# A two-layer diffusion trunk on one core: low parts of 28 second-layer weight chunks made one block earlier, and three modulations moved to TensorE

## The chip, the core and the metric

The kernel runs on one core of one Trainium2 chip. The core has TensorE for matrix products (PE, with its weight loads listed as PEld), VectorE (DVE), ScalarE (ACT), GpSimd (POOL) and SyncE (SP); here SP issues nearly all transfers, in the order in which they stand in its queue. Every engine works through its own instructions in the order of the program and waits for others on semaphores. The metric is the device time of one execution, in microseconds (us).

## The reference

Two layers of a diffusion trunk are computed for one sequence of 256 latent tokens and one of 256 context tokens, 1024 channels, all in float32. From a condition vector six modulations of 1024 values come per layer, `silu(c) @ w_ada + b_ada`. They shift, scale and gate:

```python
hl = modulate(x, ml[..., 0, :], ml[..., 1, :])
zl = hl @ w_in[l] + b_in[l]            # 1024 x 7680: q, k, v, conv, pool, gates
...
x = layer_norm(DEEPNORM_ALPHA * x + ml[..., 2, :] * mix(zl, attn_l), ln1_g[l], ln1_b[l])
x = layer_norm(DEEPNORM_ALPHA * x + ml[..., 5, :] * ffn(modulate(x, ml[..., 3, :], ml[..., 4, :])), ...)
```

`mix` joins attention, a 31-tap depthwise convolution branch and a pooling branch by gates and multiplies by `w_out`. `ffn` is `w_up` (1024 x 5632), a 3-tap depthwise convolution, a gate, and `w_down` (2816 x 1024). The first layer does all of it for both sequences. The second needs of the context only keys and values.

## The kernel before

**Weights are streamed.** All weights lie in memory as chunks of 128 x 1024 float32 (512 KB), in the order of the list `ORDER`. An item of it is ("conv", layer, j, half), ("kv", ...), ("q", ...), ("up", ...), ("down", ...) and so on. `load_to` issues the loads on SP some items ahead of their use (`LA` = 6) into six buffers called `raw`. A product in float32 is made of three products in a faster format, lines 362 to 364: high part of the one by high part of the other, low by high, high by low. So each chunk is split: ACT copies it to the short format (`hi`, line 260), and DVE subtracts (`lo = raw - hi`, line 261). `split_to` does this three chunks ahead of use, into five `hi` and five `lo` buffers. In the first layer one matmul covers 512 columns (both sequences), in the second 256 for most weights.

**Stages.** For each layer: 16 conv chunks, 4 kv, 8 q, then gates, pooling, attention and the output product; a layer norm; 44 up chunks; 22 down chunks; a layer norm. The 31 taps of the convolution (line 649, tiles `H`) are DVE work in the background. `run_bg` hands out a set number of them at each step (`NTAPS`), at a lower priority, so that a scheduler may put them later, and the order on DVE is then fixed when the program is built.

**Modulations** are made in two ways. `ada` (line 309) is a TensorE product: four matmuls of 32 columns by 256 for each of 8 chunks, then a copy of the row (DVE, line 315) and two transposes (line 343). `adt` (line 331) is a DVE product that is summed on the way, once or twice per chunk, from two buffers called `rawt`. `_ADA` and `_ADT` say which modulation is made how and in which phase. `adt` items are put in a list `due` as the use of the stream passes them, and `run_due` works them off, in the feed-forward blocks of the first layer. `take_ada` takes the modulation items that stand next in the stream, at a layer norm.

**Layer norms.** Residual sums are transposed (line 429), DVE takes means and variances, the normed tiles are transposed back (line 468), and ACT and DVE make the modulated high and low parts (`hh` line 500, `hl` line 505), which the first matmuls of the next stage need. The first three chunks of that stage are taken before the norm.

## Time and profile before

| what | value |
|---|---|
| median of 3 runs (lowest, highest) | 1458.98 us (1457.18, 1460.99) |
| profiled execution: its time / its span from first to last instruction | 1459.06 us / 1457.3 us |
| PE busy, share of the span | 1397.7 us, 96% |
| DVE busy | 1097.2 us, 75% |
| ACT busy | 700.4 us, 48% |
| mean granted TensorE clock | 0.987 |

The prediction cuts the span into stages, by the times at which tiles of that stage appear: the first feed-forward block's norm and up part (539 to 805), the norm before the second layer (923.3 to 945.7), its conv chunks (945.7 to 989.6), kv (989.6 to 1012.2), q and the start of attention (1012.2 to 1061.7), and gates, pooling and attention (1061.7 to 1171.5); its norm before the up part lies at 1242.5 to 1257. A window row gives for each engine the busy time in that stretch and the count of instructions, then the granted clock, the share of the 16 DMA engines and GB/s. Busy PE is not PE at its peak: it also counts pipelined time, so the count of matmuls per stretch is read beside it.

### The profile page before, as it was taken

How to read it: one execution, taken by the hardware profiler on the slowest of the kernel's cores; microseconds unless marked ns; L12 is line 12 of the kernel's file. 1: busy time of each engine (PE TensorE's matmuls, PEld its weight loads, DVE VectorE, ACT ScalarE, POOL GpSimd, SP SyncE). 2: the span in 40 equal slices, each digit the busy share in tenths (PEclk: the TensorE clock that was granted, in tenths of full speed). 3: DMA queues.
4: the chain of work that ended last, by engine and by line, in shares of the span. 5: the costliest groups of instructions: out<-in, count | busy, mean ns of one | idle time of the engine just before them, and what ended most of it. 6: DMA issues, size and time to landing. Idle time of an engine off the chain costs nothing. (4 is left out here: it accounts for less than half of the span.)

```text
span 1457.3 us, 21593 instructions
## 1 busy us (share of the span) xinstructions
PE 1397.7 (96%) x8340; PEld 1209.6 (83%) x8340; DVE 1097.2 (75%) x1999; ACT 700.4 (48%) x1162; POOL 62.0 (4%) x61
## 2 busy tenths in 40 slices
PE   7999899999999999999999999889799989899997
PEld 5777678888877898888888888887678989899997
DVE  3598896986994757777765866699999968777753
ACT  3332356554738437333333222643576765655542
POOL 0020320000000000000000000000400000000000
PEclk9999999999999999999999999999989999999999
DMA  9543332323232521444442777344323345355550
GB/s 365 208 178 132 111 109 73 94 101 100 98 122 94 187 88 71 155 153 150 159 153 82 254 245 241 114 144 165 121 95 124 123 160 188 129 181 183 177 171 29
DMA packets 64550, 212.28 MB, mean 146 GB/s; under 512 B 7360, under 2 KB 8512, under 8 KB 64320
## 3 DMA queue, kind: packets, MB, share of 16 engines
q1 hardware_dynamic: 62320, 207.95, 41.8%
q10 hardware_dynamic: 2128, 2.96, 0.6%
q8 instruction: 65, 1.06, 0.3%
q14 instruction: 37, 0.30, 0.1%
HBM read 209.83 MB, written 1.05 MB: 145 GB/s over the span
## 5 line engine op out<-in xcount | busy, mean ns | idle before, releaser
L260 ACT ACTIVATE hi<-raw 128x1024 fp32r<-128x1024 f32 (+2 forms) x295 | 303.8, 1034 | 481.9 <-PE mm L363 361.3
L261 DVE TENSOR_TENSOR lo<-raw,hi 128x1024 fp32r<-128x1024 f32 (+2 forms) x295 | 352.6, 1199 | 132.9 <-ACT hi L260 127.8
L363 PE MATMUL mm<-hl,hi 128*128 128x256 f32 (+1 forms) x1112 | 352.3, 319 | 2.5 <-DVE hl L505 2.4
L362 PE MATMUL mm<-hh,hi 128*128 128x256 f32 (+1 forms) x1112 | 348.1, 320 | 6.5 <-ACT sg L671 3.2
L364 PE MATMUL mm<-hh,lo 128*128 128x256 f32 (+1 forms) x1112 | 350.9, 317 | 2.7 <-DVE lo L261 2.7
L649 DVE SCALAR_TENSOR_TENSOR H<-gl,vt,H 128x502 f32<-128x502 f32 (+29 forms) x480 | 267.2, 614 | 0.1
L362 PEld LDWEIGHTS mm<-hh,hi 128*128 128x128 f32 x1112 | 211.4, 193 | 22.2 <-ACT sg L671 3.6
L363 PEld LDWEIGHTS mm<-hl,hi 128*128 128x128 f32 x1112 | 214.2, 193 | 18.2 <-DVE hl L505 3.8
L364 PEld LDWEIGHTS mm<-hh,lo 128*128 128x128 f32 x1112 | 214.2, 193 | 16.5 <-DVE lo L261 2.9
L362 PE MATMUL mm<-hi,hi 128*128 128x512 f32 x464 | 186.1, 401 | 0.0
L364 PE MATMUL mm<-hi,lo 128*128 128x512 f32 x368 | 144.5, 393 | 1.4 <-DVE lo L261 1.4
L363 PE MATMUL mm<-xlo,hi 128*128 128x512 f32 x368 | 144.0, 391 | 0.0
L362 PE MATMUL mm<-ah,hi 128*128 128x256 f32 (+1 forms) x374 | 123.1, 329 | 0.0
L364 PE MATMUL mm<-ah,lo 128*128 128x256 f32 (+1 forms) x374 | 122.8, 328 | 0.0
L363 PE MATMUL mm<-al,hi 128*128 128x256 f32 (+1 forms) x374 | 122.3, 327 | 0.0
L331 DVE CUSTOM_DVE_ANT_0 prod<-rawt,cb,vt 128x1024 f32<-128x1024 f32 x80 | 102.5, 1282 | 17.5 <-DMA rawt<-in_wst 16.6
L362 PEld LDWEIGHTS mm<-hi,hi 128*128 128x128 f32 x464 | 87.8, 189 | 25.0 <-issue 5.7
L364 PEld LDWEIGHTS mm<-hi,lo 128*128 128x128 f32 x368 | 69.1, 188 | 16.8 <-DVE lo L261 2.2
L363 PEld LDWEIGHTS mm<-xlo,hi 128*128 128x128 f32 x368 | 69.2, 188 | 13.9 <-issue 0.4
L364 PEld LDWEIGHTS mm<-ah,lo 128*128 128x128 f32 x374 | 71.1, 190 | 6.1
L363 PEld LDWEIGHTS mm<-al,hi 128*128 128x128 f32 x374 | 71.1, 190 | 6.0
L362 PEld LDWEIGHTS mm<-ah,hi 128*128 128x128 f32 x374 | 71.1, 190 | 5.9
(197 smaller groups left out, 2065.3 us busy)
## 6 DMA issues: line engine op xcount, KB each, us to landing
raw<-in_wst SPq DMA_DIRECT2D x296, 512.0 KB, 3.6
rawt<-in_wst SPq DMA_DIRECT2D x56, 512.0 KB, 4.1
ad<-in_wst SPq DMA_DIRECT2D x32, 256.0 KB, 6.0
raw<-in_wst SPq DMA_DIRECT2D x16, 384.0 KB, 3.2
x<-in_xT SPq DMA_DIRECT2D x8, 256.0 KB, 6.3
raw<-in_wst SPq DMA_DIRECT2D x8, 256.0 KB, 2.6
x<-in_xT ACTq DMA_DIRECT2D x8, 256.0 KB, 3.1
bq<-in_brow SPq DMA_DIRECT2D x6, 256.0 KB, 3.5
```

The costliest lines, as they stand in the source:

```text
L260: pin(A.activation(hi[:, :w], r[:, :w], AF.Copy))
L261: pin(V.tensor_tensor(lo[:, :w], r[:, :w], hi[:, :w].bitcast(F32), op=ALU.subtract))
L331: tc.keep_in_program_order(V.tensor_tensor_reduce(prod, w, cb[:, s], 1.0, col(l, "b_ada", m * 8 + c), ALU.mult, ALU.add, mods[l, m][:, c, ...
L362: pin(PE.matmul(ps, lh, rh, start=(first and i == 0), stop=False))
L363: pin(PE.matmul(ps, lh, rl, start=False, stop=False))
L364: pin(PE.matmul(ps, ll, rh, start=False, stop=(last and i == n - 1)))
L649: V.scalar_tensor_tensor(h[:, :, a:b], g[:, :, a + d:b + d], col(l, "dw_w", k * 8 + j), h[:, :, a:b], op0=ALU.mult, op1=ALU.add,)
```

## The change

**Low parts made early.** `PRE` lists the 28 chunks of layer 1's conv, kv and q. Each appears a second time in the stream, as ("pre", ...), spread over the up part of layer 0's feed-forward block: it is loaded there into a `rawt` buffer (three now), ACT makes its high part (in a `hi` buffer), DVE overwrites the chunk with its low part, and SP stores that to a scratch tensor in memory (`scr`). In layer 1, `split_to` then loads the low part from there instead of having DVE subtract it. The high part is made by ACT from the weights as before. `run_due` has a second place in the up loop.

**Modulations.** (0,5), (1,2) and (1,5) go from `adt` to `ada`. They are put behind the first three chunks of the up part of layer 0, of the conv of layer 1 and of the up part of layer 1, so `take_ada` takes them at the layer norms. (1,0), which is made for both sequences, goes from the up to the down part. `adt` products in the up part are 16 instead of 48, in the down part 32 as before.

**Buffers.** Five `raw` and three `rawt` instead of six and two; outside the stretch that has side items (`adt`, `pre`), the stream uses all eight in turn. Loads run 8 items ahead instead of 6.

```diff
-NRAW = 6
-NRAWT = 2
-LA = 6
+NRAW = 5
+NRAWT = 3
+LA = 8
...
-_ADA = {(0, "mix"): ((0, 2), (0, 4), (0, 3))}
-
-_ADT = {(0, "up"): ((0, 5), (1, 1), (1, 0)), (0, "down"): ((1, 2), (1, 4), (1, 3), (1, 5))}
+_ADA = {(0, "mix"): ((0, 2), (0, 4), (0, 3)), (0, "up"): ((0, 5),), (1, "conv"): ((1, 2),), (1, "up"): ((1, 5),)}
+
+_ADT = {(0, "up"): ((1, 1),), (0, "down"): ((1, 0), (1, 4), (1, 3))}
+
+PRE = [("conv", 1, j, h) for j in range(8) for h in range(2)] + [("kv", 1, k) for k in range(4)]
+PRE += [("q", 1, c, k) for c in range(2) for k in range(4)]
...
-    o = o[:GRP] + _spread(o[GRP:], ada)
+    o = o[:GRP] + ada["conv"] + _spread(o[GRP:], ada["mix"])
...
-    o += up[:GRP] + _spread(up[GRP:], adt["up"])
-    o += _spread([("down", l, c, p) for c in range(7) for p in range(3)], adt["down"])
+    o += up[:GRP] + ada["up"] + _spread(up[GRP:], _spread([("pre",) + it for it in PRE if l == 0], adt["up"]))
+    down = [("down", l, c, p) for c in range(7) for p in range(3)]
+    o += _spread(down[:18], adt["down"]) + down[18:]
...
-            if it[0] == "adt":
+            if it[0] in ("adt", "pre") or (not side(nxt["load"]) and nxt["load"] % (NRAW + NRAWT) >= NRAW):
                 t = wp.tile([P, CH], F32, tag="rawt", name=f"rawt{nxt['load']}", bufs=NRAWT)
...
             pin(A.activation(hi[:, :w], r[:, :w], AF.Copy))
-            pin(V.tensor_tensor(lo[:, :w], r[:, :w], hi[:, :w].bitcast(F32), op=ALU.subtract))
+            if it in scr:
+                load(lo[:, :w].bitcast(F32), scr.pop(it), False)
+            else:
+                pin(V.tensor_tensor(lo[:, :w], r[:, :w], hi[:, :w].bitcast(F32), op=ALU.subtract))
...
+    def pre(*it):
+
+        r = raw.pop(("pre",) + it)
+        hi = wp.tile([P, CH], F32R, tag="hi", name=uid("prehi"))
+        A.activation(hi, r, AF.Copy)
+        lo = r.bitcast(F32R)
+        tc.keep_in_program_order(V.tensor_tensor(lo, r, hi.bitcast(F32), op=ALU.subtract))
+        scr[it] = dp.tile([P, CH], F32, name=uid("scr"))
+        load(scr[it], r, False)
...
+            run_due(1)
             A.activation(acc[:, :T], acc[:, :T], AF.Silu)
```

The instructions move with it, in the order in which they stand on each engine. In these rows L362 to L364 before are L393 to L395 after, L261 is L281, L649 is L680, L673 is L704, L429 and L468 are L460 and L499, and L202 is L210.

**PE, from the last down product of layer 0 into layer 1's first conv chunks** (`ah`, `al`: activations; `sT`: residual sums; `nat`: normed tiles; `hh`: the modulated input). Before:

```order
L364 MATMUL mm940_7785<-ah908_6976,lo267_7678 128x256
L468 MATMUL ax950_7974<-ID_76,nat915_7186 128x128 x4
L468 MATMUL ax957_7993<-ID_76,nat927_7413 128x128 x2
L429 MATMUL ax948_7965<-ID_76,sT941_7852 128x128
L429 MATMUL ax948_7965<-ID_76,sT939_7747 128x128
```

After the change:

```order
L395 MATMUL mm999_7959<-ah965_7163,lo279_7858 128x256
L329 MATMUL ad1007_8144<-raw284_7855,sc_88 32x256 x3
L329 MATMUL ad1007_8144<-rawt285_7941,sc_88 32x256 x4
L329 MATMUL ad1007_8144<-rawt286_7947,sc_88 32x256 x4
L329 MATMUL ad1007_8144<-rawt287_7953,sc_88 32x256 x4
L329 MATMUL ad1007_8144<-raw288_8120,sc_88 32x256 x4
L329 MATMUL ad1007_8144<-raw289_8122,sc_88 32x256 x4
L329 MATMUL ad1007_8144<-raw290_8124,sc_88 32x256 x4
L374 MATMUL ax1009_8189<-ID_78,adarow1008_8187 128x128 x2
L460 MATMUL ax1010_8195<-ID_78,sT998_7927 128x128
```

27 of the 32 modulation matmuls and the two transposes of their row now stand between the last product and the norm's transposes, which the next stage's input waits for; the other five stand a little ahead, in the last product.

**DVE, in layer 1's conv chunks** (`gl`: the gated conv input; `H`: taps). Before:

```order
L261 TENSOR_TENSOR lo284_8595<-raw284_8485,hi284_8594 128x1024
L673 SCALAR_TENSOR_TENSOR gl1013_8625<-mm1010_8567,vt1_81,sg1012_8623 128x256
L261 TENSOR_TENSOR lo285_8653<-raw285_8516,hi285_8652 128x1024
L649 SCALAR_TENSOR_TENSOR H984_8166<-gl982_8131,vt1_81,H984_8166 128x247 x2
L649 SCALAR_TENSOR_TENSOR H984_8166<-gl982_8131,vt1_81,H984_8166 128x246 x2
L649 SCALAR_TENSOR_TENSOR H984_8166<-gl982_8131,vt1_81,H984_8166 128x245 x2
```

After the change:

```order
L704 SCALAR_TENSOR_TENSOR gl1075_8855<-mm1072_8797,vt1_83,sg1074_8853 128x256
L680 SCALAR_TENSOR_TENSOR H1046_8396<-gl1044_8361,vt1_83,H1046_8396 128x243 x2
L680 SCALAR_TENSOR_TENSOR H1046_8396<-gl1044_8361,vt1_83,H1046_8396 128x242 x2
L680 SCALAR_TENSOR_TENSOR H1046_8396<-gl1044_8361,vt1_83,H1046_8396 128x241 x2
L704 SCALAR_TENSOR_TENSOR gl1075_8855<-mm1081_8886,vt1_83,sg1074_8853 128x256
```

The subtractions are gone here, and taps move up. In DVE's order 83 taps stood ahead of layer 1's first kv bias addition (`nat<-mm,bq`), and 104 do now; ahead of the last rotated query tile it was 104 and is 124; ahead of the first pooled tile 144 and 148; ahead of the last 246 and 246.

**SP, in layer 0's up part.** Before, weight chunks (`raw`) and modulation chunks (`rawt`) alternate:

```order
L202 DMA rawt169_5783<-in_wst 128x1024
L202 DMA raw186_6211<-in_wst 128x1024
L202 DMA rawt172_5859<-in_wst 128x1024
L202 DMA raw187_6213<-in_wst 128x1024
L202 DMA rawt175_5937<-in_wst 128x1024
```

After the change:

```order
L210 DMA scr824_5660<-rawt160_5204 128x1024
L210 DMA raw180_5842<-in_wst 128x1024
L210 DMA rawt166_5536<-in_wst 128x1024
L210 DMA scr828_5671<-rawt162_5216 128x1024
L210 DMA raw182_5875<-in_wst 128x1024
L210 DMA rawt168_5587<-in_wst 128x1024
```

Stores of low parts stand between the loads. A store waits for DVE, and the next load of the same buffer (`rawt168` takes the place of `rawt162`) waits for the store. In layer 1's conv part SP's order then has one raw chunk and one low part by turns:

```order
L210 DMA rawt301_8505<-in_wst 128x1024
L210 DMA lo296_8508<-scr863_6077 128x1024
L210 DMA rawt302_8552<-in_wst 128x1024
L210 DMA lo297_8555<-scr867_6088 128x1024
L210 DMA rawt303_8583<-in_wst 128x1024
L210 DMA lo298_8586<-scr872_6163 128x1024
```

A low part's load waits there until PE has done with the chunk five places before it, whose buffer it takes; the raw loads run eight chunks ahead.

More of the change, by code (lines that the diff above doesn't have):

```diff
@@ L92, in weight_order @@
     o += [("pw", l, c) for c in range(8)]
-    ada = [("ada", a, m, k) for a, m in _ADA.get((l, "mix"), ()) for k in range(KT)]
+    ada = {
+        ph: [("ada", a, m, k) for a, m in _ADA.get((l, ph), ()) for k in range(KT)] for ph in ("mix", "conv", "up")
+    }
     adt = {ph: [("adt", a, m, c) for a, m in _ADT.get((l, ph), ()) for c in range(KT)] for ph in ("up", "down")}
-    o = o[:GRP] + _spread(o[GRP:], ada)
+    o = o[:GRP] + ada["conv"] + _spread(o[GRP:], ada["mix"])
     o += [("wout", l, c) for c in range(8)]
     up = [("up", l, j, h) for j in range(FT) for h in range(2)]
-    o += up[:GRP] + _spread(up[GRP:], adt["up"])
-    o += _spread([("down", l, c, p) for c in range(7) for p in range(3)], adt["down"])
+    o += up[:GRP] + ada["up"] + _spread(up[GRP:], _spread([("pre",) + it for it in PRE if l == 0], adt["up"]))
+    down = [("down", l, c, p) for c in range(7) for p in range(3)]
+    o += _spread(down[:18], adt["down"]) + down[18:]
     o += [("down", l, 7, p) for p in range(3)]
@@ L118, in width @@
 def width(it):
-    if it[0] == "x":
+    if it[0] in ("x", "pre"):
         return 0
@@ L132 @@
 NWST = _o
+OFFSET.update((("pre",) + it, OFFSET[it]) for it in PRE)
 @with_exitstack
@@ L143, in trunk @@
     st = ctx.enter_context(tc.tile_pool(name="st", bufs=4))
+    dp = ctx.enter_context(tc.tile_pool(name="dp", bufs=1, space=bass.MemoryType.DRAM))
     pmm = ctx.enter_context(tc.tile_pool(name="pmm", bufs=4, space=bass.MemoryType.PSUM))
@@ L213, in trunk, with side @@
     nxt = {"load": 0, "split": 0, "use": 0}
-    others = [i for i, it in enumerate(ORDER) if it[0] not in ("ada", "adt", "ad0", "x")]
+    others = [i for i, it in enumerate(ORDER) if it[0] not in ("ada", "adt", "pre", "ad0", "x")]
+    sides = [i for i, it in enumerate(ORDER) if it[0] in ("adt", "pre")]
+    def side(i):
+        return sides[0] - LA <= i <= sides[-1]
+    scr = {}
     ahead = [([j for j in others if j > i] + [len(ORDER) - 1] * LS)[LS - 1] for i in range(len(ORDER))]
@@ L231, in load_to @@
                 continue
-            if it[0] == "adt":
+            if it[0] == "pre":
+                w = CH
+            if it[0] in ("adt", "pre") or (not side(nxt["load"]) and nxt["load"] % (NRAW + NRAWT) >= NRAW):
                 t = wp.tile([P, CH], F32, tag="rawt", name=f"rawt{nxt['load']}", bufs=NRAWT)
@@ L245, in split_to @@
             load_to(n)
-            if it[0] in ("ada", "adt", "ad0", "x"):
+            if it[0] in ("ada", "adt", "pre", "ad0", "x"):
                 continue
@@ L270, in take @@
             split_to(i if strict else ahead[i])
-            if ORDER[i][0] not in ("ada", "adt") and unfinished:
+            if ORDER[i][0] not in ("ada", "adt", "pre") and unfinished:
                 unfinished.pop(0)()
@@ L276, in take @@
                 ada(*ORDER[i][1:])
-            elif ORDER[i][0] == "adt":
-                due.append(ORDER[i][1:])
+            elif ORDER[i][0] in ("adt", "pre"):
+                due.append(ORDER[i])
     def take_ada():
-        while ORDER[nxt["use"]][0] in ("ada", "adt"):
+        while ORDER[nxt["use"]][0] in ("ada", "adt", "pre"):
             i = nxt["use"]
@@ L289, in take_ada @@
             else:
-                due.append(ORDER[i][1:])
+                due.append(ORDER[i])
         while unfinished:
@@ L337, in run_due @@
         for _ in range(min(n, len(due))):
-            adt(*due.pop(0))
+            it = due.pop(0)
+            (adt if it[0] == "adt" else pre)(*it[1:])
+    def pre(*it):
[6 more added lines that the diff above has]
+        load(scr[it], r, False)
     def ada_end(l, m, row):
@@ L1141, in _lay_out @@
         kind, l = it[:2]
-        if kind == "x":
+        if kind in ("x", "pre"):
             continue
```

## The prediction, made before the changed kernel ran

> **What bounds the kernel now.** I read the page's first part and its slices first, then cut the span into stages with the view of windows, then read the groups of single lines inside each stage.
>
> ```profile
> span 1457.3 us, 21593 instructions
> PE 1397.7 (96%) x8340; PEld 1209.6 (83%) x8340; DVE 1097.2 (75%) x1999; ACT 700.4 (48%) x1162; POOL 62.0 (4%) x61
> PE   7999899999999999999999999889799989899997
> DVE  3598896986994757777765866699999968777753
> ```
>
> PE is busy nearly everywhere, but DVE reads nine tenths or more in slices 27 to 32 (984 to 1166 us), which is layer 1's mix. Windows show what that means (each row: stretch; its length; busy time and count of PE, PEld, DVE, ACT, POOL; granted clock; DMA share; GB/s):
>
> ```profile
> 570.00:805.00 235.00, 235.00 (x1059) 195.44 (x1058) 166.85 (x227) 90.12 (x116) 0.00 (x0) 1.00 0.41 140
> 945.70:989.60 43.90, 38.78 (x293) 38.06 (x293) 42.24 (x83) 21.33 (x29) 3.58 (x4) 0.92 0.44 150
> 989.60:1012.20 22.60, 22.07 (x99) 18.13 (x99) 21.22 (x46) 4.15 (x6) 0.00 (x0) 1.00 0.41 140
> 1012.20:1061.70 49.50, 38.04 (x219) 32.83 (x217) 46.73 (x84) 26.15 (x78) 20.15 (x16) 0.95 0.38 124
> 1061.70:1078.70 17.00, 17.00 (x94) 13.57 (x95) 13.82 (x37) 13.26 (x25) 0.00 (x0) 0.86 0.33 120
> 1078.70:1171.50 92.80, 92.43 (x671) 84.53 (x670) 92.78 (x245) 69.19 (x112) 0.00 (x0) 1.00 0.35 114
> 1290.00:1320.00 30.00, 30.00 (x253) 30.00 (x252) 20.86 (x31) 17.14 (x27) 0.00 (x0) 1.00 0.52 181
> ```
>
> Layer 0's up part (first row) is PE's: no idle, DVE at 71%. Layer 1's conv part (second) is DVE's: 42.24 of 43.9, while PE idles 5.1 us and its granted clock falls to 0.92. Its 293 matmuls cover 256 columns, as those of layer 1's up part do (last row, 30.00/253 = 0.119 us each), so PE needs 293 x 0.119 = 34.7 us. The kv part is PE's own (22.07 of 22.6). In the q part DVE holds again: 46.73 of 49.5, PE idle 11.5. The long stretch from 1078.7 has DVE full and PE reading busy to 0.4 us.
>
> **Gain 1: subtractions leave layer 1's mix.** 28 of them go. The line's time in those windows, and that of the taps (L649):
>
> ```profile
> L261 DVE TENSOR_TENSOR lo<-raw,hi 128x1024 fp32r<-128x1024 f32 (+2 forms) x295 | 352.6, 1199 | 132.9 <-ACT hi L260 127.8
> L649 DVE SCALAR_TENSOR_TENSOR H<-gl,vt,H 128x502 f32<-128x502 f32 (+29 forms) x480 | 267.2, 614 | 0.1
> 945.70:989.60 43.90, 13.38 (x12) 0.92 0.44 150
> 989.60:1012.20 22.60, 7.18 (x6) 1.00 0.41 140
> 945.70:989.60 43.90, 20.38 (x46) 0.92 0.44 150
> 1012.20:1061.70 49.50, 17.97 (x41) 0.95 0.38 124
> ```
>
> (The third and fourth rows are the conv and kv windows for L261 alone, the last two conv and q for L649 alone.) A tap there costs 20.38/46 = 0.443 us.
>
> Conv: all 12 subtractions fall away; in their order on DVE about two more taps come in. DVE: 42.24 - 13.38 + 2 x 0.443 = 29.7 us, less than PE's 34.7. The stage then belongs to PE with some loss, since the products wait in turn for the gate's last operand; I take 38.4 us, a gain of **5.5** (bounds: 43.9 - 34.7 = 9.2, and nothing).
>
> Kv: **0**; PE was full, and 19 more taps fit where 6 subtractions (7.18) were.
>
> Q: 8 subtractions (8 x 1.199 = 9.6) leave. 104 taps stand ahead of the first kv addition where 83 stood, and 148 ahead of the first pooled tile where 144 stood, so between the two there are 44 instead of 61: 17 x 17.97/41 = 7.4 us fewer, done in the room that the subtractions left in conv and kv. DVE: 46.73 - 9.6 - 7.4 = 29.7. PE's 38.04 at clock 0.95 are 36.1 at full clock; POOL's 20.15 belong to the rotation of keys and queries, a chain in series with DVE, ACT and PE. Next late is PE or that chain; I take 39.0, a gain of **10.5** (bounds 49.5 - 36.1 = 13.4, and nothing).
>
> 1061.7 to 1078.7: PE full at clock 0.86; at 1.00 it would take 14.6. With no idle of PE ahead of it the clock should hold: **2.0** (0 to 2.4).
>
> 1078.7 to 1171.5: 246 taps stand ahead of the last pooled tile before and after, 144 and now 148 ahead of the first, so 4 taps leave: 4 x 0.438 = **1.8**. The 23 other subtractions stay. That is all this DVE-full stretch gets, since the freed DVE time earlier is bounded by when the conv inputs exist.
>
> Sum of gains: 5.5 + 10.5 + 2.0 + 1.8 = 19.8.
>
> **The work put into layer 0's up part.** In: 28 subtractions (33.6 us of DVE) and 28 copies (28 x 1.034 = 29.0 of ACT). Out: 32 `adt` products.
>
> ```profile
> L331 DVE CUSTOM_DVE_ANT_0 prod<-rawt,cb,vt 128x1024 f32<-128x1024 f32 x80 | 102.5, 1282 | 17.5 <-DMA rawt<-in_wst 16.6
> L260 ACT ACTIVATE hi<-raw 128x1024 fp32r<-128x1024 f32 (+2 forms) x295 | 303.8, 1034 | 481.9 <-PE mm L363 361.3
> rawt<-in_wst SPq DMA_DIRECT2D x56, 512.0 KB, 4.1
> raw<-in_wst SPq DMA_DIRECT2D x296, 512.0 KB, 3.6
> out_x<-o SPq DMA_DIRECT2D x2, 256.0 KB, 2.3
> 840.00:870.00 30.00, 30.00 (x137) 24.59 (x136) 20.55 (x34) 7.10 (x8) 0.00 (x0) 1.00 0.74 248
> 600.00:630.00 30.00, 30.00 (x134) 24.82 (x134) 22.24 (x31) 10.65 (x14) 0.00 (x0) 1.00 0.45 158
> ```
>
> DVE: 166.85 - 32 x 1.282 + 33.6 = 159.4 of 235. ACT: 90.12 + 29.0 = 119.1. DMA: 36 side loads (28 and 8) stand where 24 stood, and 28 stores come in: 40 x 0.524 MB = 21.0 MB more, over 235 us 89 GB/s on top of 140, so 229. The down part after it (840 to 870) moved 248 GB/s at 137 matmuls in 30 us, no fewer than the 134 of 600 to 630 with 158. So this costs **0** while the ring of three `rawt` buffers keeps up: 36 items in 3 buffers over 235 us give a buffer 235 x 3/36 = 19.6 us a turn, and a turn needs 4.1 (load) + 1.03 + 1.20 + a store, which no row shows at this size: between 2.3 (half the size) and the load's 4.1, so 8.6 to 10.4, and I take 10.4. If this cover is gone, the excess falls on SP's queue, in which a store waits for DVE and the raw loads of the stream stand behind it (rival D).
>
> **Three modulations on TensorE at the norms.** What one costs, and where PE waits at the norms:
>
> ```profile
> 449.93 1.50 PE L309 MATMUL ad<-raw,sc 128*32 128x256 f32 x24
> L343 PE MATMUL ax<-ID,adarow 128*128 128x128 f32 x6 | 1.5, 331 | 4.1 <-DVE adarow L315 4.1
> 926.01 0.55 PE L429 MATMUL ax<-ID,sT 128*128 128x128 f32 x3 [1.89 <-DVE sT L480]
> 927.71 1.23 PE L362 MATMUL mm<-hh,hi 128*128 128x256 f32 x4 [0.91 <-ACT hh L500]
> 1247.31 2.88 PE L468 MATMUL ax<-ID,nat 128*128 128x128 f32 x12 [3.72 <-DVE nat L457]
> 539.00:568.00 29.00, 25.16 (x193) 22.81 (x192) 21.59 (x49) 20.78 (x38) 0.69 (x1) 1.00 0.21 73
> 923.30:945.70 22.40, 18.14 (x129) 17.41 (x127) 14.48 (x36) 18.48 (x35) 0.69 (x1) 0.85 0.22 72
> 1242.50:1257.00 14.50, 10.32 (x71) 9.81 (x71) 10.26 (x26) 10.52 (x21) 0.69 (x1) 0.88 0.20 73
> ```
>
> A matmul of this line leaves two records, so 24 are three chunks: 0.50 us a chunk, 4.0 a modulation. Its two transposes wait for the row's copy (4.1 over three modulations, 1.4 each) and take 0.5.
>
> Norm of layer 1's mix input (923.3): 27 of 32 matmuls, the wait and the transposes stand ahead of the residual sums' transposes: 27/32 x 4.0 + 1.4 + 0.5 = 5.3, less the 1.89 that PE waited inside anyway, is 3.4. ACT's chain (18.48 of 22.4 busy) sets much of this stage, and PE's later idle of 2.4 takes up some: **+2.5** (0 to 5.3).
>
> Norm of layer 1's up part: the modulation's 4.0 + 1.4 + 0.5 = 5.9 fall in the stall of 3.72 before the back transposes, 2.2 at the plain sum: **+2.0** (-1.7, if PE kept busy there holds its clock, which lost 0.12 x 14.5 in that window; to 5.3 as above).
>
> Norm of layer 0's up part: two back transposes go first, the rest waits for PE, idle here for 29.0 - 25.16 = 3.84: 5.9 - 3.84 = 2.1 less what lies under ACT: **+1.5** (0 to 6.0, since chunks 5 to 7 are loaded only after chunks 0 to 2 gave up their buffers).
>
> Sum +6.0 (-1.7 to +16.6). Their 24 chunk loads, in `raw` and `rawt` buffers on SP, come where DMA share is 0.20 to 0.22, so they add nothing but that wait for buffers. The `adt` products they replace save nothing: PE sets the pace of the up part, and the down part keeps 32.
>
> **Transfers in layer 1's conv.** A chunk is 24 matmuls there (8 blocks of columns, three products), 24 x 0.119 = 2.85 us, and now two loads, 1.05 MB: 368 GB/s at PE's own pace. The most that the trace shows, and a stretch in the stream:
>
> ```profile
> 0.00:30.00 30.00, 22.08 (x225) 15.77 (x226) 12.54 (x35) 10.72 (x15) 0.44 (x8) 1.00 0.96 361
> 810.00:840.00 30.00, 30.00 (x137) 24.58 (x136) 22.73 (x39) 6.18 (x8) 0.00 (x0) 1.00 0.80 269
> ```
>
> At 361 a pair takes 2.90, so the 293/24 = 12 pairs lose 12 x 0.05 = 0.6 us; eight chunks of lead cover that: **0**. On SP a low part's load waits for PE to leave its buffer five chunks back, which gives it 4 x 2.85 = 11.4 us where a load takes 4.1, and the raw loads queued behind it are eight chunks, 22.8 us, ahead. At 269 they would not (rival C). [...]
>
> **The sum.** 1459.06 (the profiled execution, 0.08 above the median of the runs, its span 1457.3) - 19.8 + 6.0 = 1445.3, taken as 1445. A measurement of this kernel tells about 0.3% (4.4 us) from no change.
>
> **Rivals.** B, PE's pace everywhere: conv 34.7 and q 36.1 are reached and the norms hide the modulations: -9.2 - 13.4 - 2.4 - 1.8 = -26.8, 1432. For it: DVE has room (29.7 in both). Against: a chain in q through POOL, and waits at the norms. C, another resource takes DVE's place: if loads run at 269 GB/s, as at 810 to 840 where 0.80 of the engines were busy, the conv part's 12 pairs are 12.6 MB, 47 us, 3 more than now instead of 5.5 less: 1445 + 8.5 = 1454. The same time comes if the rotary chain holds the q part at 48. Against: the 810 row is what was asked for, not a limit, as PE lost nothing. D, slower: the ring in layer 0's up part. It costs from the point at which a buffer's turn passes 19.6 us, and decides the sign from 21, twice the summed 10.4: each of 12 turns then loses 1.4, +17, 1462; at a turn of 22, 12 x 2.4 = +29, 1474. For it: DVE's subtraction stands in line behind the background taps and the rest, a store's length is not in the trace, and both hold SP's queue. Against: nearly twofold room. E, the conv and q stages end with something not seen, so that gains and norm costs cancel: 1459. For it: the DVE-full stretch from 1078.7 gets only 4 taps fewer.
>
> **How the numbers follow.** Forecast (6 to 20 us faster, 1439 to 1453) 0.50; B 0.08; C 0.22, half of it beyond the bound of 0.3%; D 0.15; E 0.05. Faster: 0.50 + 0.08 + 0.11 = 0.69; same: 0.11 + 0.05 = 0.16; slower 0.15. The range takes in B, C and E and leaves D's 0.15 out: 1431 to 1460; for the forecast alone 1439 to 1453.
>
> **What would show it.** In the changed kernel's windows: no subtraction of conv, kv or q chunks in layer 1; the conv part 38 us with DVE near 30 and clock near 1.0 instead of 0.92; kv unchanged at 22.6; the q part near 39 with DVE near 30, and PE or POOL as the releaser of what waits; the stretch to the last pooled tile 91 instead of 92.8. Layer 0's up part with 134 matmuls in 30 us as now, DMA near 0.67 of share; one `rawt` turn of about 10 us. Norms longer by 1.5, 2.5 and 2.0 us. It is wrong if PE waits for `lo` loads from the scratch tensor in conv (C), if PE shows idle for `raw` in layer 0's up part with SP behind a store (D), or if q keeps its length with POOL's or ACT's chain in it (C). It is wrong in the sum, not in the mechanism, if the norms cost over 10 us together.

## The result, and the profile after

The changed kernel takes 1441.18 us (median of 4 runs, 1439.88 to 1442.56) where the kernel before took 1459.99 beside it (1457.18 to 1462.77): a ratio of 0.9871, 95% interval 0.9849 to 0.9894. It is 18.8 us faster; 14 had been forecast, with a range of 1431 to 1460.

The profiled execution has a span of 1438.1 us, 19.2 less than before. To see where they come from, the span is cut at events that the timeline of both kernels shows: the first and last gated tile of the up part (`acc`), the last residual sum (`sT`), the first product that uses `hh`, the first kv product, the first gate (`g`), the last pooled tile. Each stretch is read from one execution of each kernel.

| stretch | before, us | after, us | difference |
|---|---|---|---|
| start to the first gated tile, layer 0's up part | 575.6 | 576.3 | +0.7 |
| up and down part of layer 0, to its last residual sum | 349.9 | 348.3 | -1.6 |
| norm: to layer 1's first product with `hh` | 2.2 | 9.0 | **+6.8** |
| to the first kv product | 60.8 | 53.2 | **-7.6** |
| to the first gate | 73.2 | 53.7 | **-19.5** |
| to the last pooled tile | 109.8 | 109.6 | -0.2 |
| to the last residual sum of the mix | 71.0 | 70.9 | -0.1 |
| norm: to the first gated tile, layer 1's up part | 18.2 | 20.5 | **+2.3** |
| to the end | 196.6 | 196.3 | -0.3 |

The first row scatters by itself: over all the kernels of this document it lies between 574.6 and 578.6, so its +0.7 tells nothing. Further on, a stretch that an edit does not touch comes out alike (from the first kv product to the first gate, 53.7 to 53.9 us in eight kernels).

The windows of the changed kernel that answer to those shown of before are these (same columns: busy time and count of PE, PEld, DVE, ACT, POOL; granted clock; DMA share; GB/s). The first is layer 0's up part, then the norm, then layer 1's conv, kv, q, the 16 us after it and the DVE-full stretch, by the same events as before; only the norm's row starts later than its row of before, at the last residual sum (925.5 in the kernel before):

```profile
570.00:805.00 235.00, 235.00 (x1062) 195.63 (x1061) 163.28 (x199) 116.99 (x142) 0.00 (x0) 1.00 0.65 225
924.70:951.30 26.60, 20.73 (x184) 18.27 (x179) 11.54 (x37) 18.43 (x35) 0.70 (x1) 0.94 0.66 236
951.30:988.00 36.70, 36.18 (x298) 35.97 (x299) 34.90 (x85) 21.01 (x30) 6.32 (x4) 1.00 1.02 387
988.00:1005.80 17.80, 17.80 (x81) 14.66 (x80) 17.31 (x46) 4.24 (x6) 0.00 (x0) 1.00 0.65 241
1005.80:1040.60 34.80, 34.78 (x193) 30.07 (x191) 30.42 (x57) 23.91 (x76) 16.87 (x16) 1.00 0.74 255
1040.60:1057.00 16.40, 16.40 (x112) 14.18 (x113) 15.12 (x42) 15.15 (x28) 0.00 (x0) 1.00 0.31 100
1057.00:1150.30 93.30, 93.30 (x677) 85.46 (x676) 92.83 (x242) 68.77 (x110) 0.00 (x0) 1.00 0.36 119
```

Conv, kv and q now run at PE's pace: PE idles 0.5 us in the three together, and the clock is 1.00 where it had been 0.92 and 0.95. DVE is still busy for 34.90 of 36.7 us in conv and 17.31 of 17.8 in kv, with 60 and 40 taps where 46 and 33 stood, but PE no longer waits for it. The long stretch behind them is as DVE-full as it was. In layer 0's up part PE does three instructions more than before in the same 235 us, with the DMA engines at 0.65 instead of 0.41. The norm is the one place that grew much.

### The profile page after: what moved, and what is told of

It reads as the page before. It is cut to its first block, busy times and chain, and to the rows that moved or that the text cites. A ratio compares the mean times of both kernels' runs of the same rounds, so it can differ in the third digit from the quotient of the medians.

```text
span 1438.1 us, 22130 instructions
## 1 busy us (share of the span) xinstructions
PE 1400.5 (97%) x8538; PEld 1207.9 (84%) x8538; DVE 1056.9 (73%) x1941; ACT 728.1 (51%) x1190; POOL 64.4 (4%) x59
## 4 chain that ended last, share of the span: by engine, by line
PE 73%; issue 20%; DVE 3%; ACT 2%; POOL 2%; DMA 1%; SPq 0%; POOLq 0%; ACTq 0%
PE mm L393 21%; PE mm L394 21%; PE mm L395 20%; PE ax L427 3%; PE ax L891 1%; PE ad L329 1%; PE ax L460 1%; PE ax L499 1%; POOL gc L721 1%; PE ax L393 1%; DVE lo L281 1%; PE ax L395 1%; PE ax L394 1%; PE ad L571 1%; DMA rt<-in_rope 1%
## 5 line engine op out<-in xcount | busy, mean ns | idle before, releaser
L277 ACT ACTIVATE hi<-raw 128x1024 fp32r<-128x1024 f32 (+2 forms) x212 | 218.5, 1038 | 281.5 <-PE mm L394 206.6
L393 PE MATMUL mm<-hh,hi 128*128 128x256 f32 (+1 forms) x1112 | 346.7, 317 | 8.1 <-ACT hh L531 4.6
L395 PE MATMUL mm<-hh,lo 128*128 128x256 f32 (+1 forms) x1112 | 349.5, 316 | 0.0
L281 DVE TENSOR_TENSOR lo<-raw,hi 128x1024 fp32r<-128x1024 f32 (+1 forms) x193 | 229.9, 1194 | 100.6 <-ACT hi L277 96.7
L680 DVE SCALAR_TENSOR_TENSOR H<-gl,vt,H 128x502 f32<-128x502 f32 (+29 forms) x480 | 264.5, 606 | 0.1
L393 PEld LDWEIGHTS mm<-hh,hi 128*128 128x128 f32 x1112 | 209.5, 191 | 23.4 <-ACT hh L531 5.1
L395 PEld LDWEIGHTS mm<-hh,lo 128*128 128x128 f32 x1112 | 212.1, 191 | 13.9 <-issue 1.1
L393 PE MATMUL mm<-hi,hi 128*128 128x512 f32 x464 | 186.1, 401 | 0.0
L395 PE MATMUL mm<-hi,lo 128*128 128x512 f32 x368 | 144.5, 393 | 1.1 <-DVE lo L281 1.1
L277 ACT ACTIVATE hi<-rawt 128x1024 fp32r<-128x1024 f32 (+2 forms) x83 | 84.9, 1025 | 114.0 <-PE mm L394 60.3
L393 PE MATMUL mm<-ah,hi 128*128 128x256 f32 (+1 forms) x374 | 123.2, 329 | 0.0
L395 PE MATMUL mm<-ah,lo 128*128 128x256 f32 (+1 forms) x374 | 122.8, 328 | 0.0
L281 DVE TENSOR_TENSOR lo<-rawt,hi 128x1024 fp32r<-128x1024 f32 (+2 forms) x74 | 86.9, 1177 | 34.4 <-ACT hi L277 34.2
L393 PEld LDWEIGHTS mm<-hi,hi 128*128 128x128 f32 x464 | 87.8, 189 | 25.0 <-issue 5.7
L395 PEld LDWEIGHTS mm<-hi,lo 128*128 128x128 f32 x368 | 69.1, 188 | 16.4 <-DVE lo L281 1.9
L395 PEld LDWEIGHTS mm<-ah,lo 128*128 128x128 f32 x374 | 71.1, 190 | 6.1
```

The costliest lines, as they stand in the source:

```text
L277: pin(A.activation(hi[:, :w], r[:, :w], AF.Copy))
L281: pin(V.tensor_tensor(lo[:, :w], r[:, :w], hi[:, :w].bitcast(F32), op=ALU.subtract))
L393: pin(PE.matmul(ps, lh, rh, start=(first and i == 0), stop=False))
L395: pin(PE.matmul(ps, ll, rh, start=False, stop=(last and i == n - 1)))
L680: V.scalar_tensor_tensor(h[:, :, a:b], g[:, :, a + d:b + d], col(l, "dw_w", k * 8 + j), h[:, :, a:b], op0=ALU.mult, op1=ALU.add,)
```

## The experiments

Four kernels change the work at layer 1's norm, three put modulations elsewhere, four take the change apart, and one changes a size. The kernel before ran beside them, with medians of 1458.2 to 1459.4. Times of neighbouring kernels differ by little (the intervals of their ratios to before partly overlap), so the readings rest on the lengths of the stretches in the traces, cut as in the table above.

**What makes the norm long.** In the changed kernel, ACT and PE do this there (start, length, engine, line, operation, and in brackets the idle time before it and what ended it):

```profile
925.75 1.06 ACT L277 ACTIVATE hi<-raw 128x1024 fp32r<-128x1024 f32 x1 [2.91 <-DMA raw<-in_wst]
931.62 1.06 ACT L277 ACTIVATE hi<-raw 128x1024 fp32r<-128x1024 f32 x1 [4.81 <-DMA raw<-in_wst]
932.58 0.58 ACT L462 ACTIVATE nat<-ax 128x512 f32<-128x512 f32 x1
933.05 0.56 ACT L531 ACTIVATE hh<-ax,sBn,sAn 128x256 fp32r<-128x256 f32 x1
```

```profile
928.32 0.44 PE L374 MATMUL ax<-ID,adarow 128*128 128x128 f32 x2 [0.54 <-DVE adarow L335]
928.59 0.60 PE L460 MATMUL ax<-ID,sT 128*128 128x128 f32 x4
929.03 1.04 PE L499 MATMUL ax<-ID,nat 128*128 128x128 f32 x8
933.66 1.22 PE L393 MATMUL mm<-hh,hi 128*128 128x256 f32 x4 [3.60 <-ACT hh L531]
```

PE has done the transposes by 930.1, but ACT stands in a weight copy until 932.7. In ACT's order two copies, of the conv chunks (1,1,1) and (1,2,0), come ahead of the norm's `nat` and `hh`. The load of (1,2,0) takes a buffer that a modulation chunk held, so it is issued only after TensorE has used that chunk, at 925.24, and it lands 6.3 us later, where the median `raw` load of this kernel takes 4.3. The DMA engines are full at that time:

```profile
921.00:927.00 6.00, 6.00 (x79) 4.92 (x80) 0.56 (x2) 2.90 (x4) 0.00 (x0) 1.00 0.94 350
927.00:933.00 6.00, 2.53 (x28) 1.72 (x20) 0.97 (x6) 1.38 (x2) 0.00 (x0) 1.00 1.00 328
```

The first try at it:

```diff
             load_to(i + LA)
-            split_to(ahead[i])
+            if ORDER[i][:3] != ("ada", 1, 2):
+                split_to(ahead[i])
```

> Edit: the changed kernel, but while (1,2)'s eight items are taken at layer 1's norm the next conv chunks are not split, so their ACT copies stand behind the norm's work instead of ahead of it. My theory: of the 6.4 us by which that norm grew, 3.6 us are PE's wait for hh (933.66 us in the trace after), because ACT stands in its copy of conv chunk (1,2,0), whose load waits for a buffer that a modulation chunk holds. Then 1441.2 - 3.6 = 1437.6 us. Rival: the modulation's own PE work ahead of the transposes (27 matmuls, wait for the row, transposes, 5.3 us by the prediction's rows) is the cost, and the ACT copy's wait lies inside it: 1441 us, or a little more because copies collide with the hh chain on ACT.

It took 1442.19 us (1441.22 to 1443.3). That settled nothing: the scheduler put the copies where they had been, and PE still waited 2.46 us for `hh`. The edit that does move them gives the two copies an order behind the fourth `hh` (and, not shown here, splits no chunk beyond conv's first three until the modulation's items have been passed):

```diff
+            if it in (("conv", 1, 1, 1), ("conv", 1, 2, 0)):
+                tc.add_manual_dep(
+                    cp.ins, hlog[2][3].name, mybir.DependencyInfo(mybir.DependencyClass.NoSync, mybir.DependencyReason.DATA),
+                    reason="order of copies",
+                )
```

> Edit: the changed kernel, with ACT's copies of conv chunks (1,1,1) and (1,2,0) ordered behind the fourth hh of layer 1's norm. (The kernel of the run e5 had left both ahead of the norm: in its trace ACT still waits 3.27 us for a raw chunk there, so it told nothing apart.) My theory: PE's wait of 3.6 us for hh comes from ACT standing in the copy of (1,2,0), whose load waits for a modulation chunk's buffer. With the copies behind, nat and hh start when the transposes end, at 930 us instead of 933: 1441.2 - 3.1 = 1438.1 us. Rival: the copies are then missing later, on an ACT that is busy with the hh chain, and the conv part gives the 3 us back: 1441 us.

It took 1436.89 us (1436.66 to 1437.52). In its trace (its lines stand some 11 higher) ACT goes straight from the wait for PE to `nat` and `hh`, and PE's wait for `hh` is 0.27 us:

```profile
929.26 0.60 ACT L473 ACTIVATE nat<-ax 128x512 f32<-128x512 f32 x1 [6.39 <-PE ax L471]
929.75 0.56 ACT L543 ACTIVATE hh<-ax,sBn,sAn 128x256 fp32r<-128x256 f32 x1
930.36 0.62 PE L404 MATMUL mm<-hh,hi 128*128 128x256 f32 x3 [0.27 <-ACT hh L543]
```

The norm is 5.7 us instead of 9.0, and the conv part gives back 0.3 (53.5 for 53.2). So 3.3 us of the norm's 6.8 were ACT standing in order behind a late load. The rest would be the modulation's own PE work ahead of the transposes. To test that, the next kernel adds to e6 that `take_ada` is called after `modulated` at layer 1's norm and at its up part's norm:

```diff
-            take_ada()
             r.feed(7, ps, 1)
             r.modulated(0, *aff, hs, xs, NTOK, SEQ)
+            take_ada()
```

> Edit: the kernel of the run e6 (ACT's copies of two conv chunks behind the norm's hh), and the modulations (1,2) and (1,5) asked for after the norm's modulated parts instead of ahead of them, so that their TensorE work lies between the products that wait for hh. My theory: what is left of the norms' cost, 5.7 - 2.2 = 3.5 us at layer 1's norm and 1.8 at its up part's norm, is the modulation's matmuls, row copy and transposes ahead of the norm's transposes on PE. Behind them they lie under ACT's hh chain, which PE waits for anyway: 1436.9 - 5.3 + about 1.5 for what is not covered = 1433 us. Rival: PE is full from the first hh on, and the 4.0 us of each come back a little later: 1437 us.

It took 1434.29 us (1433.42 to 1434.95), ratio 0.9839 (0.9824 to 0.9853), the fastest kernel here. From the last residual sum to the first kv product it needs 55.6 us, where e6 needed 59.2 and the kernel before 63.0: the 3.5 us came at that place. They show in the conv part (50.1 instead of 53.5), since the first `hh` product comes hardly earlier (5.5 us after the sum instead of 5.7): most of the modulation's matmuls still stand ahead of it, now behind the norm's transposes. At the other norm nothing came (20.4 us, as in e6), although the transposes of the modulation's row and some of its matmuls moved behind there too. What sets that norm is read in the next section. A further kernel on e6 only left out the forced end of the modulation:

```diff
-        while unfinished:
-            unfinished.pop(0)()
```

> Edit: the kernel of the run e6, and the two transposes of a modulation's row are no longer forced ahead of the norm's transposes; at layer 1's norm they come some 40 products later, the matmuls stay where they were. My theory: of the 3.5 us left at that norm, the wait for the row's copy (0.5 in the trace after) and the transposes (0.4), with DVE's copy between them, are about 1.4: 1435.5 us. Rival: PE has to wait for the last matmul's partner anyway, so nothing changes: 1437 us.

It took 1438.2 us (1437.64 to 1438.37). The norm was 4.8 us instead of 5.7, but conv took 54.0 instead of 53.5, with the clock at half for 3.4 us at 934, which it is not in e6. Of the 1.4, then, at most 0.9 came, and 0.4 in sum: the larger part of the 3.5 lies in the matmuls, not in the row's transposes. That it is slower than e6 comes from another place, the clock behind the last pooled tile (last section).

**Modulations elsewhere.**

```diff
-_ADA = {(0, "mix"): ((0, 2), (0, 4), (0, 3)), (0, "up"): ((0, 5),), (1, "conv"): ((1, 2),), (1, "up"): ((1, 5),)}
+_ADA = {(0, "mix"): ((0, 2), (0, 4), (0, 3)), (0, "up"): ((0, 5),), (1, "mix"): ((1, 2),), (1, "up"): ((1, 5),)}
```

> Edit: modulation (1,2) spread over layer 1's mix (conv to pooling weights) instead of its norm; (0,5) and (1,5) stay at norms. My theory: the 6.4 us at the norm go away, both the PE part and the ACT copy's wait, and the 4.0 us of PE work come back in the mix only in part, as PE's waits for kT and qT there (2 to 3 us per 30) take some: 1437 us (1435 to 1439). Rival: layer 1's mix is at PE's pace now, so the modulation's 4.0 us and the wait for its row (1.4) come back in full: 1440 us or more.

It took 1438.48 us (1437.77 to 1438.96). The norm is at 2.2 us again, so all 6.8 go with the modulation. But the stretch from kv to the first gate grew by 2.2, the next by 0.4 and the one behind the last pooled tile by 1.7: 4.3 in all, as much as the 4.0 of the modulation's matmuls. The time lies in the theory's range, yet its "only in part" is not what the stretches show; of the rival, the 4.0 came and the further 1.4 for the row did not. Why the growth is not spread as the matmuls are (16 and 8 of their 64 records in the two stretches that grew most) stays open.

```diff
+_ADA = {(0, "mix"): ((0, 2), (0, 4), (0, 3)), (0, "up"): ((0, 5),)}
+_ADT = {(0, "up"): ((1, 1), (1, 0)), (0, "down"): ((1, 2), (1, 4), (1, 3), (1, 5))}
```

> Edit: (1,2) and (1,5) are DVE products in layer 0's down part again, and (1,0) in the up part, as before the change; (0,5) stays at its norm; low parts and buffers as in the change. Side items in layer 0's up part: 44 instead of 36. My theory: the two norms get back 6.4 + 2.1 = 8.5 us, and the up part stays at PE's pace, as a buffer's turn of 235 x 3/44 = 16.0 us is still over the 10.4 that a turn needs: 1441.2 - 8.5 = 1432.7 us. Rival: three buffers and DVE's room in the up part are then used up (DVE 159.4 + 16 x 1.28 = 180 of 235, plus waits in SP's queue), and the up part grows by what the norms give back or more: 1441 to 1450 us.

It took 1436.09 us (1434.37 to 1439.02), between the two. The norms gave back what was expected (2.2 and 18.2 us, as before the change). Layer 0's up and down part took 351.1 us instead of 348.3. The up part itself has no idle PE; the loss is in the last down chunks, where PE waits for ACT's copy (1.69 us) and DVE's subtraction (0.76). A further 1.4 us lie behind the last pooled tile, where the clock fell for 3.4 us (last section). To remove the wait for the copy, the products were spread over fewer down chunks:

```diff
-    o += _spread(down[:18], adt["down"]) + down[18:]
+    o += _spread(down[:15], adt["down"]) + down[15:]
```

> Edit: the kernel of the run e1 (modulations (1,2) and (1,5) back as DVE products), with the 32 product items of layer 0's down part spread over its first 15 chunks instead of 18. My theory: in e1, 2 to 3 us were lost near 915 us, where PE waits for copies of the last down chunks, whose loads wait for the last products' buffers. With the products done three chunks earlier that wait goes: 1436.1 - 2.4 = 1433.7 us. Rival: DVE cannot keep up with 32 products in 15 chunks, and the same wait stands earlier: 1436 us or more.

It took 1454.21 us (1452.4 to 1457.74). The rival was right and too mild: PE waits 15.06 us, until 896, for ACT's copy of a down chunk. A wait of this kind comes up in the next two kernels, and its cause is shown for the second.

**The change taken apart.**

```diff
-PRE = [("conv", 1, j, h) for j in range(8) for h in range(2)] + [("kv", 1, k) for k in range(4)]
-PRE += [("q", 1, c, k) for c in range(2) for k in range(4)]
+PRE = []
-    o += up[:GRP] + ada["up"] + _spread(up[GRP:], _spread([("pre",) + it for it in PRE if l == 0], adt["up"]))
+    o += up[:GRP] + ada["up"] + _spread(up[GRP:], adt["up"])
```

> Edit: the changed kernel without any low part made early (no side items for it, all 28 subtractions in layer 1 again); the three modulations and the buffers as in the change. My theory: the norms' costs are seen alone, +0.3 + 6.4 + 2.1 = +8.8 over the kernel before, of which layer 1's mix gives nothing back: about 1468 us. Rival: the norm of layer 1 was long because the loads of the low parts filled the DMA engines (0.94 to 1.00 of share there): without them it costs some 3.6 us less, 1464 us. Second rival: nothing at the norms matters, as DVE's backlog sets layer 1's mix anyway: 1460 us.

It took 1478.05 us (1476.38 to 1480.33), more than any theory said. Up and down part of layer 0 take 362.8 us instead of 349.9: PE waits 11.29 us at 903 for ACT's copy of a down chunk, as in e9. The norms, read by themselves, cost +4.4 (to the first `hh` product) and +2.2. From the first `hh` product to the first gate the kernel needs 131.5 us, where the change needs 107.0 and the kernel before 134.0. So 24.5 of the mix's 27.0 us belong to the low parts, and without their loads layer 1's norm grows by 2.4 us less than the 6.8 (the first rival had said 3.6).

```diff
-_ADA = {(0, "mix"): ((0, 2), (0, 4), (0, 3)), (0, "up"): ((0, 5),), (1, "conv"): ((1, 2),), (1, "up"): ((1, 5),)}
+_ADA = {(0, "mix"): ((0, 2), (0, 4), (0, 3))}
-_ADT = {(0, "up"): ((1, 1),), (0, "down"): ((1, 0), (1, 4), (1, 3))}
+_ADT = {(0, "up"): ((0, 5), (1, 1), (1, 0)), (0, "down"): ((1, 2), (1, 4), (1, 3), (1, 5))}
```

(with the edit of e2 as well)

> Edit: the kernel before with the change's buffers and load distance (five raw, three rawt, in turn; 8 items ahead; the second place for side work in the up loop; DVE products spread over 18 of 21 down chunks), no low parts, no modulation moved. My theory: nothing before the change waited for loads, so 1458 us within 3. Rival: without low parts the three rawt buffers let the last down chunks wait, as in the run with the modulations alone (11.5 us of PE waiting for a copy of a down chunk near 890 us there): 1465 us or more.

It took 1477.94 us (1476.13 to 1478.8), 18.5 slower than before: what is left of the change here (the buffers and their turns, the load distance, the spread of the products) is a loss by itself. The wait shows as such on SP (loads; here the length is that of the whole group), ACT and PE:

```profile
864.41 6.67 SPq L209 DMA_DIRECT2D rawt<-in_wst  x4
871.17 0.38 SPq L209 DMA_DIRECT2D raw<-in_wst  x1
876.56 33.34 SPq L209 DMA_DIRECT2D rawt<-in_wst  x13
910.44 1.46 SPq L209 DMA_DIRECT2D raw<-in_wst  x2
```

```profile
905.80 1.06 ACT L276 ACTIVATE hi<-rawt 128x1024 fp32r<-128x1024 f32 x1 [14.08 <-DMA rawt<-in_wst]
906.91 0.80 PE L392 MATMUL mm<-ah,hi 128*128 128x512 f32 x1 [15.92 <-ACT hi L276]
```

Thirteen loads into `rawt` stand in a row on SP. Most are modulation chunks, which wait for DVE to finish earlier ones, and DVE's products stand behind residual sums that wait for PE; the last are the stream's own down chunks, which PE waits for. To show that it is these chunks' use of `rawt`, and not the load distance or the spread, the next kernel is e3 without one condition:

```diff
-            if it[0] in ("adt", "pre") or (not side(nxt["load"]) and nxt["load"] % (NRAW + NRAWT) >= NRAW):
+            if it[0] in ("adt", "pre"):
```

> Edit: the kernel of the run e3 (buffers alone, 1477.9 us), but the stream's chunks never take a rawt buffer: five raw buffers for them all through. My theory: the 15.9 us for which PE waits near 890 us in e3 come from the first down chunk that takes a rawt buffer in turn, whose load stands behind 13 loads of product chunks on SP, and those wait for DVE products that stand behind residual sums. Without turns that wait goes: 1460 us, or a few more because five buffers serve the whole kernel. Rival: the turns are not it, but the load distance of 8 or the spread of the products over 18 chunks: 1475 us or more, with the same wait.

It took 1457.23 us (1455.73 to 1461.1), ratio to before 0.9994 (0.9981 to 1.0007), and between 840 and 925 us PE's longest wait is this:

```profile
PE ax L459 <- DVE sT L510: 0.4, 1, 0.4
```

The turns are the cause. In the change the last down chunks take `rawt` buffers too. There ACT's last copy ahead of the gap starts at 881.5 and the next at 903.5, and PE's store of split chunks just covers it; in e3 the copies start at 864.7 and 905.8. Why the order on SP came out three chunks better in the change was not tried.

**How the gain depends on which low parts are made.**

```diff
-PRE = [("conv", 1, j, h) for j in range(8) for h in range(2)] + [("kv", 1, k) for k in range(4)]
+PRE = [("kv", 1, k) for k in range(4)]
```

> Edit: the changed kernel, low parts made early for kv and q only (12 chunks); the 16 conv chunks are subtracted in layer 1. My theory: DVE's work sets each stage down to PE's counted floor. The conv part is back at 60.8 us from first hh to first kv product (53.2 in the change), and the stretch from there to the first gate, 73.2 before and 53.7 in the change, loses 12 x 1.2 = 14.4 us and keeps the taps that conv could not take: 58.8. Sum: 1441.2 + 7.6 + 5.1 = 1454 us. Rival 1: the subtractions held PE there by being late themselves, so that 12 fewer give all of that stretch's gain: 53.7 us, 1449 us in all. Rival 2: mere count, 12 of 28 of the gain of 25: 1455.5 us, with the gain spread over the mix.

It took 1453.08 us (1449.35 to 1456.83; its profiled execution has a span of 1453.0). Its conv part and the stretch from kv to the first gate:

```profile
932.00:994.30 62.30, 54.63 (x409) 53.08 (x410) 53.88 (x117) 35.77 (x58) 4.03 (x5) 0.92 0.50 175
994.30:1055.10 60.80, 56.17 (x279) 48.01 (x277) 52.50 (x113) 29.28 (x82) 18.55 (x16) 0.94 0.70 236
```

Conv is back at 62.3 (60.8 before). The second stretch is 60.8, near the 58.8 of the stage-wise account; rival 1 (53.7) falls. Rival 2's total (1455.5) is not told apart by the time, but its even spread is: conv gained nothing, and all that was gained lies between kv and the first gate. Of the 7 us between 60.8 and the change's 53.7, 4.6 are DVE time of taps that conv did not take (72 taps here, 62 in the change); PE waits 4.62 us at one place there, and the clock is at half for 6.8.

**The room in layer 0's up part.**

```diff
-NRAW = 5
-NRAWT = 3
+NRAW = 6
+NRAWT = 2
```

> Edit: the changed kernel with six raw and two rawt buffers instead of five and three. My theory: a side item's turn in layer 0's up part is load 4.3 + copy 1.03 + subtraction 1.2 + store 4.4 = 10.9 us by the groups of the changed kernel, and two buffers give 235 x 2/36 = 13.1: the up part stays at PE's pace (226 us from first to last gated product), and the time within 3 us of 1441. Rival: waits in order on ACT, DVE and SP's queue add to the turn more than the 2.2 us that are left, so the up part grows: at a turn of 15, 18 x 1.9 = 34 us more, 1475.

It took 1441.2 us (1439.76 to 1442.96), the same as the change, and its up part (first to last gated tile) has no idle PE:

```profile
578.60:804.70 226.10, 226.10 (x999) 187.14 (x998) 158.30 (x190) 109.11 (x133) 0.00 (x0) 1.00 0.67 230
```

Even two buffers, 13.1 us a turn, are enough: rival D's place was in no danger.

## Why the prediction was right, and where its steps were off

The direction, the range and the mechanism of the gain held (1439 to 1453 for the forecast alone). Two errors lay in the sum and partly cancelled: the gain was 7.0 us larger, the norms cost 3.4 more, and 1.6 came from layer 0's up and down part.

**Conv, -5.5 forecast, -7.2 measured** (43.9 to 36.7). PE sets it as said. The loss over the counted 34.7 was 2.0, not 3.7. DVE's 29.7 was wrong: not two but 14 more taps came in (60 for 46), and it is busy for 34.90. PE idles only 0.5 us all the same.

**Kv, 0 forecast, -4.8; q, -10.5 forecast, -14.7**, more than its stated bound of 13.4. This is the step that failed: "PE was full" and "38.04 at clock 0.95 are 36.1" took all that PE was busy with between two marks as work that has to be done between them. The conv step had used counts instead. In kv and q together the busy time gave a floor of 22.07 + 36.1 = 58.2 us; the changed kernel passes the same marks in 17.8 + 34.8 = 52.6, with 81 + 193 = 274 PE instructions where 318 had stood. By kind of product the difference is plain. The products of kv and q themselves are 191 in the two windows before and 188 after. The products for the chunks behind q are 96 before and 56 after (one of their three kinds, in the q window before and after):

```profile
L362 PE MATMUL mm<-hh,hi 128*128 128x256 f32 x32 | 9.1, 285 | 0.0
L393 PE MATMUL mm<-hh,hi 128*128 128x256 f32 x19 | 5.5, 292 | 0.0
```

At 0.119 us each the 40 are 4.8 of the 5.6 us. They stood ahead of the first score product (`ax<-kT,qT`) in PE's order, and stand behind it now. The mark between kv and q, an event of DVE, moved against PE's work as well: 95 of the 96 kv products lay ahead of it in the old window, and in the changed kernel 14 of them come behind it. So kv's -4.8 and q's -14.7 are not gains of two stages; only what comes of all windows together counts.

**The 17 us after q, -2.0 forecast, -0.6.** The clock is 1.00 there, as forecast, but 18 more PE instructions fell into it, of those that had stood in q's window. **The DVE-full stretch, -1.8 forecast, +0.5**: DVE is 92.83 of 93.3 busy, and the four taps that left were made up for by one more subtraction and by small work.

Together -26.8 where -19.8 was forecast. It is by chance the figure of rival B for the mix (-26.8); B's other half, norms that hide the modulations, is wrong.

**Layer 0's up part, 0 forecast.** Right: 226.9 us before and 226.4 after from first to last gated tile, with DVE at 163.28 in 235 us (159.4 forecast), ACT 116.99 (119.1), 225 GB/s (229). The stores and the loads of low parts, by the changed kernel's list of DMA issues (count, size, median us from issue to landing):

```profile
scr<-rawt SPq DMA_DIRECT2D x28, 512.0 KB, 4.4
lo<-scr SPq DMA_DIRECT2D x28, 512.0 KB, 6.0
```

A store is just over the upper bound of 4.1 that the prediction took, and no PE wait came of it.

**The norms, +6.0 forecast, +9.4 measured** (0.7 + 6.4 + 2.3). Layer 0's norm by itself, from the mix's last residual sum to the first gated tile, is 27.3 us in the kernel before (27.3 and 27.4 in e12 and e3, which have no modulation there either) and 28.3 in the change (28.0 to 28.9 in the others that have it): +1.0 where 1.5 was forecast. Layer 1's up norm, +2.3 for 2.0, came out right by luck. Forecast was PE work of the modulation in a stall of PE. In the traces ACT sets the pace there, working without a gap from the first normed tile to the first `hh`: two weight copies now stand among the normed tiles in its order, ahead of the first `hh` (before, then after):

```profile
1246.93 2.08 ACT L453 ACTIVATE nat<-nat,nm,lrs 128x256 f32<-128x256 f32 x4 [2.71 <-DVE nm L446]
1248.91 0.55 ACT L500 ACTIVATE hh<-ax,sBm,sAm 128x256 fp32r<-128x256 f32 x1
```

```profile
1226.22 1.04 ACT L277 ACTIVATE hi<-raw 128x1024 fp32r<-128x1024 f32 x1
1227.17 1.08 ACT L484 ACTIVATE nat<-nat,nm,lrs 128x256 f32<-128x256 f32 x2
1228.28 1.06 ACT L277 ACTIVATE hi<-raw 128x1024 fp32r<-128x1024 f32 x1
1229.25 0.59 ACT L484 ACTIVATE nat<-nat,nm,lrs 128x256 f32<-128x256 f32 x1
1229.74 0.55 ACT L531 ACTIVATE hh<-ax,sBm,sAm 128x256 fp32r<-128x256 f32 x1
```

The first `hh` starts 6.4 us after the last residual sum before the change and 8.5 after it. In e10, with the row's transposes moved away, it is still 8.4, with the same two copies ahead. That moving them would give the 2 us back was not tried.

Layer 1's mix norm was +2.5 with an upper bound of 5.3, and measured 6.4 to the first gate of its conv part (`sg`; 20.2 us before from the last residual sum, 26.6 after). The price of the modulation's PE work was right by its rows (5.3 - 1.89 = 3.4; without the blocked copy it is 5.7 - 2.2 = 3.5, e6), and the discount from there to 2.5 was not. What was left out is that the chunk loads of the modulation take buffers from the stream. The prediction said of them that they "add nothing but that wait for buffers" because the DMA share was 0.20 to 0.22, and gave the wait for buffers a price at layer 0's norm only. At this norm the share rose to 0.94 to 1.00, a copy ahead of the norm in ACT's order waited for such a buffer, and 3.3 us followed (e6).

**Transfers in conv.** Rival C falls: no PE wait for a low part appears. Two loads per chunk were carried at 387 GB/s over 36.7 us. The 361 of the first 30 us, which the prediction used as the most that the trace shows, was not the limit.

## What to carry to other kernels

Floors are counted, not read from busy time: the instructions that belong to the stage, by kind, at the duration of the same shape in a stretch where nothing waits. Busy time between two marks can hold work of the next stage (here 40 products, 4.8 us), and the marks move when the order changes, so the parts behind one bottleneck must be summed over all of them.

When work is put into an idle gap, list what its transfers displace. A copy for later work that stands in order ahead of urgent work turns a late load into a stall (here 3.6 us of PE); letting it stand behind was worth 3 us, putting the added matmuls behind the urgent ones as much again. Sharing buffers between a stream and side work that waits for the stream can cost more (18.5 us) than the buffers give.

## What the runs showed of the chip that was not expected

**One core's transfers.** 387 GB/s over 36.7 us, with 512 KB a load, and up to 429 in a slice of 0.92 us:

```profile
GB/s 388 348 344 344 402 420 420 411 411 411 339 364 286 246 348 397 429 400 397 411 420 411 402 411 415 411 397 415 420 406 397 424 384 402 366 417 380 397 321 388
```

(the conv part of the changed kernel in 40 slices of 0.92 us). The most that the prediction had found in the trace before was 361, over the first 30 us.

**The clock falls in steps of 3.4 us, and not at every wait of the same length.** In the kernel before, layer 1's mix had stretches at half clock behind its waits, such as these two; the changed kernel has one such stretch between 850 and 1420 us, at its norm:

```profile
964.20:967.60 3.40, 3.04 (x14) 3.05 (x15) 3.40 (x6) 0.00 (x0) 0.00 (x0) 0.50 0.48 154
1056.30:1066.50 10.20, 6.80 (x19) 4.37 (x19) 7.51 (x16) 3.44 (x7) 0.00 (x0) 0.50 0.33 104
```

```profile
933.20:936.60 3.40, 2.94 (x13) 2.94 (x14) 2.50 (x10) 1.90 (x4) 0.70 (x1) 0.50 0.95 349
```

So a part of the gain in the mix is the clock that idle PE had lost. In e10 the clock also fell behind the last pooled tile, where PE waits 1.95 us for ACT; e6 has the same wait and keeps the clock.

The traces show what decides. In each of the 14 traces the stretches at half clock begin whole multiples of 3.413 us apart (in the kernel before those at 926.6, 947.1, 964.2, 1056.3 and 1247.5 lie 6, 5, 27 and 56 of them apart, 320.85 us in all), as if time were cut into fixed windows. By these windows e10's wait lies in one (first row; the second is the one at half clock), and e6's is cut by an edge (last two rows):

```profile
1161.50:1164.90 3.40, 1.45 (x14) 1.21 (x12) 1.22 (x1) 3.36 (x5) 0.00 (x0) 1.00 0.49 153
1164.90:1168.30 3.40, 3.40 (x16) 3.40 (x17) 1.55 (x4) 3.40 (x9) 0.00 (x0) 0.50 0.46 164
```

```profile
1165.40:1168.80 3.40, 1.88 (x17) 1.64 (x15) 1.23 (x1) 2.89 (x4) 0.00 (x0) 1.00 0.55 183
1168.80:1172.20 3.40, 2.79 (x21) 2.59 (x22) 1.27 (x3) 3.40 (x8) 0.00 (x0) 1.00 0.41 154
```

PE idles 1.95 us of one window in e10, and 1.5 and 0.6 us of two in e6. Counted in this way over all 14 traces, from 200 us on and without the last 30, 36 windows at full clock are followed by one at half. PE idled for 1.88 us or more in 35 of them, and for 1.70 in one; in the 4879 that are followed by full clock it idled for at most 1.87. So about 1.9 us of idle PE in one window was the limit in these traces.

The stretch from the last pooled tile to the last residual sum is 72.1 us in e10 and 70.9 in e6. It is 72.2 to 72.5 in the others whose clock fell there once (e1, e8, e9, e11), and 73.7 in e3, where it fell twice. A kernel's time thus moves by 1.2 to 1.6 us with where such a window falls, which is to be kept in mind when e1, e6 and e11 are compared.
